# Inverse sums of the last pair of heads: spread by transfers in place of transposes on TensorE

## The chip, the cores and the metric

One core of a Trainium2 chip runs the kernel. The metric is the device time of one execution in microseconds (us); the time of a kernel is the median of several runs.

## What is computed

The reference is a decoder block with two attention branches that read one normalised input. Cut to what matters here:

```
h = rms_norm(x, norm_g)                              # x: 512 x 1024
fq, fk, fv, fz, mq, mk, mv, mz, ga, gb, fl = split(h @ w_in)
y_fox  = softmax(q k^T / 8 + c_i - c_j, causal) @ v * silu(fz)       # 8 heads of 64
y_moba = softmax(q k^T / 8 over selected blocks) @ v * silu(mz)      # 8 heads of 64
merged = sigmoid(ga + b_0) * (y_fox @ w_fox) + sigmoid(gb + b_1) * (y_moba @ w_moba)
out    = x + merged @ w_out
```

A softmax is an exponential divided by the sum of its row. The change concerns how the inverse of that sum reaches the outputs of two of the sixteen heads.

## The kernel before

Every product is made from operands split into a high and a low part, three matmuls for one. In the projections the activations are Gh and Gl and the weights wh and wl. The weights come by DMA from SP into four buffers (tag wr), ACT makes the high part (L140) and DVE the low part (L142), some products ahead of their use.

The sixteen heads are worked off in four groups of four: f/a, f/b, m/a, m/b (`attn_group`, L516). A group has two pairs of heads, and a head has these steps:

- `Aa` (L562): logits on PE (L571, L572), row maximum on DVE (L574), exponential with its row sum on ACT (L576). After the second head of a pair DVE inverts the sums into `ri` (L591), with the tokens on partitions.
- `Bb` (L609): PE transposes the exponentials (L616) into banks p_a, p_b and p_cc of tag tp, a ring of three; ACT and DVE split them (L622, L623); PE makes the outputs `pv` (L626, L627); ACT moves the half of `pv` that holds the low part of v (`ysh`, L651), and DVE adds it to the other half (L652). The outputs of a pair are one tile `ypair`, with the channels on partitions and the tokens along the row.
- `Yp` (L659): DVE multiplies `ypair` (L678) by a factor `zr`, which holds the gate ZS (silu) times the inverse sums; ACT and DVE split the result into yh and yl (L679, L680) for the projections by w_fox and w_moba.

`ypair` has the tokens along the row, so each inverse sum is needed on 64 partitions of its column. The kernel gets it there in two ways.

Seven of the eight pairs use transfers. In `sums_out` (L593), after the pair's first `Bb`, PE transposes the eight columns of `ri` into an 8x128 bank of tag tp (p_ri, L596), ACT scales it by a half (L598) and issues a write to DRAM (L599). In `sums_in` (L601) ACT issues two reads, each of which spreads one head's 512 values over 64 partitions of the tile `rinv_bc` (L606). In `Yp` GpSimd (POOL) multiplies that tile by ZS (L677).

The last pair of the last group (`last and pr`) does it otherwise, all in `Yp`: POOL copies each column of `ri` 64 times along the row (two instructions, L670, scaled by a half) into a tile rinv_w of tag u, PE transposes that tile in four pieces of 128x128 (L673) into a bank of tag lg, and DVE multiplies ZS by the bank (L674).

Around this stand the gate products. `Bb(2)` and `Bb(3)` of the last group, the tail of its list (L685), are followed by the unit wf3, and then by stage "gates" with the groups GA0, GA1 and GB0 (`group`, L722). A gate group is seven products (A11, S3, A12, S2, S1, A22, S4), each of 24 matmuls (two halves, four chunks, and three for one: L766, L768, L769). Four of the seven read sums S0 to S3 of blocks of the activations, which POOL loads back from DRAM at the start of the stage (`load_sums`, L286, eight loads at L290), into memory that the attention tiles give free. `Yp` of the last pair (`gate[0]`) is called after the third unit of GA0 (L1116).

The order on each engine isn't that of the program: a scheduler sets it with a simulated timeline, so instructions of different units are mixed. Each engine works its own list in order, and a waiting instruction holds up all behind it. DMAs are issued from the lists of SP, ACT and POOL.

Of the kernel before, what the change touches and what calls it, by code (L numbers as in the profile page):

```python
# [7 lines left out]
F32 = mybir.dt.float32  # L8
F32R = mybir.dt.float32r
AF = mybir.ActivationFunctionType  # L10
OP = mybir.AluOpType
AX = mybir.AxisListType

P = 128
S = 512
D = 1024
NT = S // P
KT = D // P
HD = 64
# [10 lines left out]
def fox_moba_kernel(ctx: ExitStack, tc, xT, x, w_in, w_fl, w_fox, w_moba, w_out, cst, rope, out):  # L30
# [3 lines left out]
    V, A, G, T = nc.vector, nc.scalar, nc.gpsimd, nc.tensor  # L34
# [6 lines left out]
    stage = {}  # L41
# [7 lines left out]
    def t2(tag, bufs, name, shape=(P, 512), dt=F32):  # L49
        pool = stage["pool"] if tag in ("qs", "pt", "pc", "ys") else sb  # L50
        return pool.tile(list(shape), dt, name=name, tag=tag, bufs=bufs)

    def pst(tag, bufs, name):
        return ps.tile([P, 512], F32, name=name, tag=tag, bufs=bufs)
# [4 lines left out]
    def tp(name):  # L59
        return pst("tp", 3, name)  # L60
# [30 lines left out]
    ident = con.tile([P, P], F32, name="ident")  # L91
# [134 lines left out]
    r = con.tile([P, NT], F32, name="r")  # L226
# [190 lines left out]
    ZS = {}  # L417
# [95 lines left out]
    ri = con.tile([P, 16, 4], F32, name="rinv")  # L513
    R_dram = dr.tile([16, NT, P], F32, name="r_dram")

    def attn_group(br, half, gq, gk):  # L516
        fox = br == "f"
        qn, kn = QN[f"{br}q{half}"], QN[f"{br}k{half}"]
        hb = 4 * (half == "b") + (0 if fox else 8)
        last = br + half == "mb"  # L520

        direct = br + half != "fa"
        st = {}
# [38 lines left out]
        def Aa(h):  # L562
            def go():
                qs, kh, kl, q2 = st[h]
                hh = hb + h
                pts = []
                for i in range(NT):
                    n = P * (i + 1)
                    lg = pst("lg", 2, "lg")
                    qt = slice(i * P, (i + 1) * P)  # L570
                    T.matmul(lg[:, :n], qs[:, qt], kh[:, :n], start=True, stop=False)  # L571
                    T.matmul(lg[:, :n], q2[:, qt], kl[:, :n], start=False, stop=True)  # L572
                    pt = stage["pool"].tile([P, n], F32, name=f"p{i}", tag=f"p{i}", bufs=2)
                    V.tensor_tensor_reduce(pt, lg[:, :n], mask[:, 512 - n:512], -0.125, 3.0e38,  # L574
                                           op0=OP.add, op1=OP.min, accum_out=mkn[:, hh, i:i + 1])
                    A.activation(pt, pt, AF.Exp, bias=mkn[:, hh, i:i + 1], scale=-1.0,  # L576
                                 accum_out=rs[:, hh, i:i + 1])
                    pts.append(pt)
                st[h] = pts
                if h % 2:  # L580
                    inverse_sums(h // 2)
                elif h:
                    sums_in(0)
            return go
# [8 lines left out]
        def sums_out(pr):  # L593
            h0 = hb + 2 * pr
            p = tp("p_ri")
            T.transpose(p[:8, :P], ri[:, h0:h0 + 2, :].rearrange("p h t -> p (h t)"), ident)  # L596
            rt = sb.tile([8, P], F32, name="rinv_t", tag="rinv_t", bufs=1)
            A.activation(rt, p[:8, :P], AF.Copy, scale=0.5)  # L598
            A.dma_start(out=R_dram[h0:h0 + 2].rearrange("h t p -> (h t) p"), in_=rt)  # L599

        def sums_in(pr):  # L601
            if last and pr:
                return
            rb = st["r", pr] = stage["pool"].tile([P, S], F32, name="rinv_bc", tag="rinv_bc", bufs=1)
            for o in range(2):
                A.dma_start(out=rb[o * HD:(o + 1) * HD, :],  # L606
                            in_=R_dram[hb + 2 * pr + o].rearrange("t p -> (t p)").partition_broadcast(HD))

        def Bb(h):  # L609
            def go():  # L610
                pts, vt = st[h], VT[f"{br}v{half}"]
                o = h % 2
                pv = pst("pv", 1, "pv")

                def blk(dst, i, j):
                    T.transpose(dst, pts[i][:, j * P:(j + 1) * P], ident)  # L616

                def spl(p, n):
                    tag, w, bufs = ("pt", 512, 4) if n == 512 else ("pc", 256, 2)
                    hi = t2(tag, bufs, "pth", (P, w), F32R)  # L620
                    lo = t2(tag, bufs, "ptl", (P, w), F32R)
                    A.activation(hi[:, :n], p[:, :n], AF.Copy)  # L622
                    V.tensor_tensor(out=lo[:, :n], in0=p[:, :n], in1=hi[:, :n].bitcast(F32), op=OP.subtract)  # L623
                    return hi, lo
                def pvm(j, hl, c0, n, start, stop):
                    T.matmul(pv[:, P * j:P * j + n], vt[:, j, h, :], hl[0][:, c0:c0 + n], start=start, stop=False)  # L626
                    T.matmul(pv[:, P * j:P * j + n], vt[:, j, h, :], hl[1][:, c0:c0 + n], start=False, stop=stop)  # L627
                pa = tp("p_a")
                for i in range(4):
                    blk(pa[:, i * P:(i + 1) * P], i, 0)  # L630
                pb = tp("p_b")
                for i in range(1, 4):
                    blk(pb[:, (i - 1) * P:i * P], i, 1)
                blk(pb[:, 384:512], 3, 3)
                ha = spl(pa, 512)
                hbb = spl(pb, 512)
                pc = tp("p_cc")
                for i in range(2, 4):
                    blk(pc[:, (i - 2) * P:(i - 1) * P], i, 2)
                hc = spl(pc, 256)  # L640
                pvm(0, ha, 0, 512, True, False)
                pvm(1, hbb, 0, 384, False, False)
                pvm(3, hbb, 384, 128, False, False)
                pvm(2, hc, 0, 256, False, True)
                pr = h // 2
                if o == 0:
                    st["y", pr] = t2("u", 4, "ypair") if last and pr else t2("ys", 1, "ypair")
                y = st["y", pr]
                me, ot = (slice(0, HD), slice(HD, P)) if o == 0 else (slice(HD, P), slice(0, HD))
                sh = t2("u", 4, "ysh")  # L650
                A.activation(sh[me, :], pv[ot, :], AF.Copy)  # L651
                V.tensor_tensor(out=y[me, :], in0=pv[me, :], in1=sh[me, :], op=OP.add)  # L652
                if o == 0 and not (last and pr):
                    sums_out(pr)
                elif pr:
                    sums_in(1)
            return go

        def Yp(pr):  # L659
            def go():  # L660
                y = st["y", pr]
                gp = 2 * (half == "b") + pr
                yh = t2("y", 15, f"yh{br}{gp}", dt=F32R)
                yl = t2("y", 15, f"yl{br}{gp}", dt=F32R)
                if last and pr:
                    zr, rb = ZS[br, gp], pst("lg", 2, "p_rinv")
                    h0 = hb + 2 * pr
                    rw = t2("u", 4, "rinv_w")
                    for o in range(2):
                        G.tensor_scalar(rw.rearrange("p (t o d) -> p t o d", o=2, d=HD)[:, :, o, :],  # L670
                                        ri[:, h0 + o, :, None].to_broadcast([P, NT, HD]), 0.5, None, op0=OP.mult)
                    for t in range(NT):
                        T.transpose(rb[:, t * P:(t + 1) * P], rw[:, t * P:(t + 1) * P], ident)  # L673
                    V.tensor_tensor(out=zr, in0=zr, in1=rb, op=OP.mult)  # L674
                else:
                    zr = st["r", pr]
                    G.tensor_tensor(out=zr, in0=ZS[br, gp], in1=zr, op=OP.mult)  # L677
                V.tensor_tensor(out=y, in0=y, in1=zr, op=OP.mult)  # L678
                A.activation(yh, y, AF.Copy)  # L679
                V.tensor_tensor(out=yl, in0=y, in1=yh.bitcast(F32), op=OP.subtract)  # L680
                Y[br, gp] = (yh, yl)
            return go
# [553 lines left out]
```

## Time and profile before

| | us |
|---|---|
| median of 3 runs | 425.06 |
| lowest, highest run | 424.13, 425.23 |
| profiled execution, its own time | 424.43 |
| its span | 422.5 |
| mean granted TensorE clock | 0.999 |

The profile shows one execution. PE is TensorE's matmuls, PEld its weight loads, DVE VectorE, ACT ScalarE, POOL GpSimd, SP the engine that only issues DMAs; ACTq is ACT's queue of DMA issues. In a timeline row stand the start in us, the length in us, the engine, the line, the operation, the output and inputs, and in brackets how long the engine was idle before and what released it. The chain that ended last has rows of start, length and instruction, each of them cut to what it adds to the chain. In the table of waits a row gives the total, the count and the longest wait in us. In the table of stretches the columns are the length, then busy time and count of PE, PEld, DVE, ACT and POOL, then the granted clock, the DMA share and GB/s.

### The profile page before, as it was taken

The numbers are of one execution on the slowest core, as the hardware profiler recorded it, in microseconds if no ns is written. First come the engines' busy times: TensorE is split into PE (matmuls) and PEld (weight loads), VectorE is DVE, ScalarE is ACT, GpSimd is POOL, SyncE is SP. The second block draws the span as 40 slices with busy tenths as digits, with TensorE's granted clock in tenths as the row PEclk, the third lists the DMA queues.
The fourth block names the chain that finished last, engine by engine and source line by source line (L and its number), as shares of the span: only waits on it lengthen the run. The fifth ranks groups of instructions, "written<-read, shape, count | busy, mean of one in ns | idle before, by whom it ended". The sixth has DMA issues, their size and how long they took to land.

```text
span 422.5 us, 7680 instructions
## 1 busy us (share of the span) xinstructions
PE 417.3 (99%) x2912; PEld 388.0 (92%) x2912; DVE 327.5 (78%) x575; ACT 279.7 (66%) x528; POOL 102.4 (24%) x120
## 2 busy tenths in 40 slices
PE   8999999999999999999999999999999999999996
PEld 6998899999999998899998888899999989988885
DVE  4669968799968779668666778767979698689883
ACT  5987327877877978569758687756655535686450
POOL 1067600224235550025650100340000000022230
PEclk9999999999999999999999999999999999999999
DMA  7982325567252123303122311673142603697494
GB/s 227 396 290 98 99 101 159 158 192 223 63 168 102 45 83 101 102 24 101 33 93 78 102 47 27 240 247 110 35 169 67 233 2 117 213 249 119 99 138 162
DMA packets 24484, 56.10 MB, mean 133 GB/s; under 512 B 2824, under 2 KB 7616, under 8 KB 24448
## 3 DMA queue, kind: packets, MB, share of 16 engines
q1 hardware_dynamic: 13536, 38.11, 28.0%
q0 software_dynamic: 3392, 8.39, 9.0%
q10 hardware_dynamic: 7520, 9.11, 6.8%
q8 instruction: 23, 0.38, 0.4%
q14 instruction: 13, 0.11, 0.1%
HBM read 48.11 MB, written 6.32 MB: 129 GB/s over the span
## 4 chain that ended last, share of the span: by engine, by line
PE 97%; DMA 1%; SPq 0%; DVE 0%; issue 0%
PE pb_GB L769 3%; PE pb_GA L769 3%; PE pb_GA L766 3%; PE pb_GB L766 3%; PE pb_GB L768 3%; PE pb_GA L768 3%; PE po L957 3%; PE po L956 3%; PE po L955 3%; PE pv L627 2%; PE lg L572 2%; PE pv L626 2%; PE lg L571 2%; PE pf L696 2%; PE pm L697 2%; PE pf L697 2%
## 5 line engine op out<-in xcount | busy, mean ns | idle before, releaser
L342 POOL TENSOR_TENSOR ff<-ss,mh 128x8 f32<-128x8 f32 x16 | 29.7, 1857 | 72.7 <-DVE ss L340 54.2
L576 ACT ACTIVATE p<-p,negm 128x128 f32<-128x128 f32 (+1 forms) x64 | 35.7, 558 | 13.0 <-DVE negm L574 12.0
L574 DVE CUSTOM_DVE_ANT_0 p<-lg,mask 128x128 f32<-128x128 f32 (+1 forms) x64 | 30.7, 485 | 15.0 <-PE lg L572 14.5
L904 POOL DMA_DIRECT2D wr_o<-in_w_out_dram x4 | 4.9, 1293 | 95.5 <-ACT wr_o L903 95.5
L142 DVE TENSOR_TENSOR wl_GA<-wr_ga,wh_GA 128x1024 fp32r<-128x1024 f32 x14 | 16.9, 1222 | 5.9 <-ACT wh_GA L140 3.9
L140 ACT ACTIVATE wh_GA<-wr_ga 128x1024 fp32r<-128x1024 f32 x14 | 14.6, 1059 | 10.1 <-PE pb_GA L768 5.1
L140 ACT ACTIVATE wh_GB<-wr_gb 128x1024 fp32r<-128x1024 f32 x14 | 14.6, 1059 | 9.5 <-PE pm L696 3.5
L571 PE MATMUL lg<-KH,QS 128*128 128x128 f32 (+1 forms) x64 | 20.4, 328 | 0.0
L918 DVE TENSOR_TENSOR wl_o<-wr_o,wh_o 128x1024 fp32r<-128x1024 f32 x14 | 17.0, 1219 | 3.8 <-ACT wh_o L917 3.8
L917 ACT ACTIVATE wh_o<-wr_o 128x1024 fp32r<-128x1024 f32 x14 | 14.8, 1060 | 7.6 <-PE pb_GB L768 2.8
L142 DVE TENSOR_TENSOR wl_GB<-wr_gb,wh_GB 128x1024 fp32r<-128x1024 f32 x14 | 16.9, 1221 | 3.5 <-ACT wh_GB L140 3.5
L652 DVE TENSOR_TENSOR ypair<-pv,ysh 64x512 f32<-64x512 f32 x16 | 11.0, 687 | 6.2 <-ACT ysh L651 5.8
L546 DVE SCALAR_TENSOR_TENSOR KL<-p_kT,cs,KH 64x512 fp32r<-64x512 f32 x16 | 12.0, 747 | 3.4 <-ACT KH L543 3.2
L623 DVE TENSOR_TENSOR ptl<-p_a,pth 128x512 fp32r<-128x512 f32 x16 | 10.9, 684 | 4.3 <-ACT pth L622 4.2
L651 ACT ACTIVATE ysh<-pv 64x512 f32<-64x512 f32 x16 | 9.5, 593 | 7.1 <-PE pv L627 4.7
L336 DVE TENSOR_REDUCE ss<-sq 128x8 f32<-128x512 f32 x16 | 10.8, 680 | 3.6 <-ACT sq L335 3.6
L766 PE MATMUL pb_GA<-Gh,wh_GA 128*128 128x256 f32 x48 | 13.5, 282 | 0.0
L768 PE MATMUL pb_GA<-Gl,wh_GA 128*128 128x256 f32 x48 | 13.5, 281 | 0.0
L769 PE MATMUL pb_GA<-Gh,wl_GA 128*128 128x256 f32 x48 | 13.5, 281 | 0.0
L769 PE MATMUL pb_GB<-Gh,wl_GB 128*128 128x256 f32 x48 | 13.5, 281 | 0.0
L768 PE MATMUL pb_GB<-Gl,wh_GB 128*128 128x256 f32 x48 | 13.4, 281 | 0.0
L766 PE MATMUL pb_GB<-Gh,wh_GB 128*128 128x256 f32 x48 | 13.3, 281 | 0.0
(461 smaller groups left out, 1794.1 us busy)
## 6 DMA issues: line engine op xcount, KB each, us to landing
wr_ga<-in_w_in_dram SPq DMA_DIRECT2D x8, 512.0 KB
wr_gb<-in_w_in_dram SPq DMA_DIRECT2D x8, 512.0 KB
wr_o<-in_w_out_dram SPq DMA_DIRECT2D x8, 512.0 KB
xt<-in_xT_dram SPq DMA_DIRECT2D x8, 256.0 KB
x<-in_x_dram SPq DMA_DIRECT2D x8, 256.0 KB
s_dramh<-sum_sh ACTq DMA_DIRECT2D x8, 256.0 KB
s_draml<-sum_sl ACTq DMA_DIRECT2D x8, 256.0 KB
wr_wf<-in_w_fox_dram SPq DMA_DIRECT2D x4, 512.0 KB
```

Source lines behind the costliest of these rows:

```text
L140: A.activation(hi[:, :, 0:n], src, AF.Copy)
L142: eng.tensor_tensor(out=lo[:, q, 0:n], in0=src[:, q], in1=hi[:, q, 0:n].bitcast(F32), op=OP.subtract)
L342: G.tensor_tensor(out=f2, in0=ss.rearrange("p t h -> p (t h)"), in1=mh, op=OP.pow)
L571: T.matmul(lg[:, :n], qs[:, qt], kh[:, :n], start=True, stop=False)
L574: V.tensor_tensor_reduce(pt, lg[:, :n], mask[:, 512 - n:512], -0.125, 3.0e38, op0=OP.add, op1=OP.min, accum_out=mkn[:, hh, i:i + 1])
L576: A.activation(pt, pt, AF.Exp, bias=mkn[:, hh, i:i + 1], scale=-1.0, accum_out=rs[:, hh, i:i + 1])
L697: T.matmul(p, lo[:, k, cc], yh, start=False, stop=(k == 3))
L766: T.matmul(o, hi[:, k, cc], lh, start=(n < 3 and c == 0 and k == 0), stop=False, skip_group_check=True)
L768: T.matmul(o, hi[:, k, cc], ll, start=False, stop=False, skip_group_check=True)
L769: T.matmul(o, lo[:, k, cc], lh, start=False, stop=(k == 3), skip_group_check=True)
L917: A.activation(wide(hi), wide(R[key, c]), AF.Copy)
L918: V.tensor_tensor(out=wide(lo), in0=wide(R[key, c]), in1=wide(hi).bitcast(F32), op=OP.subtract)
```

## The change

The last pair takes the same way as the other seven. `sums_out(1)` is called for it after `Bb(2)`, `sums_in(1)` after `Bb(3)`, and `Yp(1)` has only the branch with POOL's multiplication. The transposes of L673 and their bank, the two copies of L670 and the multiplication of L674 go. Its tile rinv_bc is taken from tag u of the pool that lasts the whole kernel, in the place of rinv_w.

```
         def sums_in(pr):
-            if last and pr:
-                return
-            rb = st["r", pr] = stage["pool"].tile([P, S], F32, name="rinv_bc", tag="rinv_bc", bufs=1)
+            rb = st["r", pr] = (t2("u", 4, "rinv_bc") if last and pr else
+                                stage["pool"].tile([P, S], F32, name="rinv_bc", tag="rinv_bc", bufs=1))
             for o in range(2):
                 A.dma_start(out=rb[o * HD:(o + 1) * HD, :],
                             in_=R_dram[hb + 2 * pr + o].rearrange("t p -> (t p)").partition_broadcast(HD))
...
-                if o == 0 and not (last and pr):
+                if o == 0:
                     sums_out(pr)
                 elif pr:
                     sums_in(1)
...
-                if last and pr:
-                    zr, rb = ZS[br, gp], pst("lg", 2, "p_rinv")
-                    h0 = hb + 2 * pr
-                    rw = t2("u", 4, "rinv_w")
-                    for o in range(2):
-                        G.tensor_scalar(rw.rearrange("p (t o d) -> p t o d", o=2, d=HD)[:, :, o, :],
-                                        ri[:, h0 + o, :, None].to_broadcast([P, NT, HD]), 0.5, None, op0=OP.mult)
-                    for t in range(NT):
-                        T.transpose(rb[:, t * P:(t + 1) * P], rw[:, t * P:(t + 1) * P], ident)
-                    V.tensor_tensor(out=zr, in0=zr, in1=rb, op=OP.mult)
-                else:
-                    zr = st["r", pr]
-                    G.tensor_tensor(out=zr, in0=ZS[br, gp], in1=zr, op=OP.mult)
+                zr = st["r", pr]
+                G.tensor_tensor(out=zr, in0=ZS[br, gp], in1=zr, op=OP.mult)
```

Behind the scheduler the lists differ only around this place. PE's list has four transposes (L673) less and one (L596) more, and the last head's transposes (L616) stand behind the outputs of the head before it and seven matmuls of GA0. ACT's has rinv_t, one write and two reads more, and yhm (L679) of the last pair stands ahead of one weight split (L140) and one copy of a bank (L776) that it stood behind. POOL's L677 stands where L670 stood. DVE's has L674 less, and L678 stands ahead of one weight split (L142) that it stood behind.

## The prediction

> **What bounds the kernel now.** I read the page first: the span, the busy shares, the span in 40 slices and the shares of the chain that ended last.
>
> ```profile
> span 422.5 us, 7680 instructions
> PE 417.3 (99%) x2912; PEld 388.0 (92%) x2912; DVE 327.5 (78%) x575; ACT 279.7 (66%) x528; POOL 102.4 (24%) x120
> PE   8999999999999999999999999999999999999996
> PE 97%; DMA 1%; SPq 0%; DVE 0%; issue 0%
> ```
>
> PE is busy in every slice between the first and the last and makes 97% of the chain. Busy alone doesn't prove that it is never held up, so the second view was the waits of PE, over the whole span:
>
> ```profile
> PE warm_ps L104 <- DVE fg_pre L479: 1.1, 1, 1.1
> PE fqa L390 <- DVE wh_fqa L163: 0.5, 1, 0.5
> ```
>
> These are all of them, and both belong to the first input tiles. From then on PE runs its list without a gap, and the chain is that list. Two things can therefore change the time: what PE has to issue, and a new wait of PE that isn't there now. Work taken from DVE, ACT or POOL is worth nothing by itself.
>
> **The change part by part.** *PE's own work.* Next come the chain's rows around the four removed transposes (start, us, what), and around one 8x128 transpose of another pair, of the kind that is added.
>
> ```profile
> 288.24 0.44 PE p_rinv L673 x4
> ...
> 255.84 0.23 PE pf L697
> 256.18 0.23 PE pf L695
> ```
>
> The four of L673 hold the chain for 0.44 us, 0.11 each. Around the 8x128 transpose (L596, which the chain leaves out as too short) one matmul ends at 255.84 + 0.23 = 256.07 and the next counts from 256.18: 0.11 for it. PE thus loses 0.44 and gains 0.11: **-0.33 us**. The Trainium skill (TensorE: Matmul & The Clock Gate, Part 4: PE-mode transpose) has a transpose inside a kernel at about 275 ns; by that the estimate would be -0.83 us. The chain's 0.44 for four speaks against it as a price on the path, since they overlap.
>
> *What the change moves on PE.* The order of the instructions, which a scheduler sets, shows more than the diff does. The added transpose takes the next bank of tag tp, a ring of three, so the last head's transposes (head 3, L616) slide back. Head 2's eight pv matmuls and seven of GA0's first product now stand ahead of them, then come the added transpose, p_a and p_b in a row, 15 gate matmuls, p_cc, 2 more, and head 3's pv. The rows that time this, of PE, ACT and DVE before:
>
> ```profile
> 275.10 0.28 PE L627 MATMUL pv<-ptl,v_mvb 128*128 128x256 f32 x1
> ...
> 278.72 0.40 PE L626 MATMUL pv<-pth,v_mvb 128*128 128x512 f32 x1
> ...
> 279.89 0.28 PE L627 MATMUL pv<-ptl,v_mvb 128*128 128x256 f32 x1
> ```
>
> ```profile
> 256.60 0.25 ACT L598 ACTIVATE rinv_t<-p_ri 8x128 f32<-8x128 f32 x1
> ...
> 275.53 0.60 ACT L651 ACTIVATE ysh<-pv 64x512 f32<-64x512 f32 x1
> ...
> 276.64 0.38 ACT L622 ACTIVATE pth<-p_cc 128x256 fp32r<-128x256 f32 x1
> ```
>
> ```profile
> 277.50 0.41 DVE L623 TENSOR_TENSOR ptl<-p_cc,pth 128x256 fp32r<-128x256 f32 x1
> ```
>
> With head 2's pv moved to the front (273.5 on, 1.3 us as head 3's take from 278.72 to 280.0), the added transpose falls at about 275.6, p_a and p_b end at 276.6, and p_cc ends at about 278.75 after 15 matmuls of 0.12. ACT does ysh (275.55 to 276.15), rinv_t (0.25), the issue of the write, two pth (to 277.8), then the pth of p_cc from 278.8 (0.38); DVE's ptl (0.41) is ready near 279.65. PE wants it for its last pv matmul, now near 280.0. A margin of 0.35 us: I cost this at nothing, and if it breaks it costs what it is over by, 0.5 us at most, as ACT has nothing else longer than that in between.
>
> *POOL.* Two copies of the sums go (L670) and one multiplication comes (L677), both behind the loads of S0 to S3 in POOL's order.
>
> ```profile
> 263.09 1.29 POOL L677 TENSOR_TENSOR rinv_bc<-zs_mzb,rinv_bc 128x512 f32<-128x512 f32 x1 [22.67 <-DMA rinv_bc<-r_dram]
> ...
> 276.03 0.54 POOL L290 DMA_DIRECT2D S2l<-s_draml  x1 [5.44 <-PE p_cc L616]
> ...
> 279.42 0.54 POOL L290 DMA_DIRECT2D S3l<-s_draml  x1 [2.33 <-PE pv L626]
> 279.98 2.67 POOL L670 TENSOR_SCALAR rinv_w<-rinv 128x256 f32<-128x256 f32 x2
> ```
>
> S2l waits for p_cc, so it goes out near 279 and not at 276.03, and S3h and S3l follow by 280.2. To land such a load takes:
>
> ```profile
> S2l<-s_draml POOLq DMA_DIRECT2D x1, 512.0 KB, 5.7
> S3h<-s_dramh POOLq DMA_DIRECT2D x1, 512.0 KB, 6.4
> ```
>
> S2l is there by 285, S3h and S3l by 286.6. PE first reads S2l at 292.16 (row below) and S3 later still: 5 us or more to spare, so nothing. After L677 POOL has no work before the output stage.
>
> *The transfers.* ACT gets rinv_t (0.25), a write of 4 KB and two reads of 128 KB. The reads stand behind ysh of head 3, which waits for pv to end; with pv over at about 280.3, the first goes out near 281.0. The write is out by 276.7, over 4 us earlier, so the reads don't wait for it. From the first read's issue to POOL's multiplication the seven other pairs give 3.6 to 5.5 us; the quickest and the slowest:
>
> ```profile
> 152.34 1.10 ACTq L606 DMA_DIRECT2D rinv_bc<-r_dram  x2
> ...
> 155.93 1.30 POOL L677 TENSOR_TENSOR rinv_bc<-zs_fzb,rinv_bc 128x512 f32<-128x512 f32 x1 [0.59 <-DMA rinv_bc<-r_dram]
> ...
> 176.20 1.11 ACTq L606 DMA_DIRECT2D rinv_bc<-r_dram  x2
> ...
> 181.73 1.28 POOL L677 TENSOR_TENSOR rinv_bc<-zs_fzb,rinv_bc 128x512 f32<-128x512 f32 x1 [20.25 <-DMA rinv_bc<-r_dram]
> ```
>
> So POOL starts between 284.6 and 286.5. I take 286.5, the upper end, because the engines of the DMA are fuller here than there (busy times by stretch; the last two columns are DMA share and GB/s):
>
> ```profile
> 278.00:282.00 4.00, 4.00 (x33) 3.90 (x32) 1.92 (x2) 2.25 (x3) 2.55 (x3) 1.00 0.99 346
> ...
> 176.00:182.00 6.00, 6.00 (x50) 5.86 (x49) 4.64 (x10) 4.66 (x12) 0.27 (x1) 1.00 0.46 131
> ```
>
> *The new waits and who stands behind them.* DVE loses L674 but its L678 now waits for POOL, with a weight split (L142) behind it; ACT's yhm (L679) waits for that L678, and behind yhm stands the split that starts group GA1.
>
> ```profile
> 286.87 1.23 DVE L142 TENSOR_TENSOR wl_GA<-wr_ga,wh_GA 128x1024 fp32r<-128x1024 f32 x1 [1.49 <-ACT wh_GA L140]
> 288.71 0.69 DVE L674 TENSOR_TENSOR zs_mzb<-zs_mzb,p_rinv 128x512 f32<-128x512 f32 x1 [0.62 <-PE p_rinv L673]
> 289.43 0.69 DVE L678 TENSOR_TENSOR ypair<-ypair,zs_mzb 128x512 f32<-128x512 f32 x1
> ```
>
> ```profile
> 289.11 1.06 ACT L140 ACTIVATE wh_GA<-wr_ga 128x1024 fp32r<-128x1024 f32 x1 [1.80 <-issue]
> ...
> 290.56 0.62 ACT L679 ACTIVATE yhm<-ypair 128x512 fp32r<-128x512 f32 x1
> ```
>
> ```profile
> 291.81 0.28 PE L766 MATMUL pb_GA<-Gh,wh_GA 128*128 128x256 f32 x1
> 291.93 0.28 PE L768 MATMUL pb_GA<-Gl,wh_GA 128*128 128x256 f32 x1
> 292.05 0.28 PE L766 MATMUL pb_GA<-S2h,wh_GA 128*128 128x256 f32 x1
> 292.16 0.28 PE L768 MATMUL pb_GA<-S2l,wh_GA 128*128 128x256 f32 x1
> ```
>
> The row at 291.81 is the first use of that split; with 0.33 less ahead of it PE is there at 291.5. Backwards from it: split 1.06, yhm 0.62, L678 0.69, POOL 1.29 and some 0.2 of hand-over make 3.9, so PE waits if POOL starts after **287.6**. At 286.5 there is 1.1 us left; L678 then runs from 287.9 and yhm from 288.6, and the split starts at 289.2 in place of 289.11. The DVE split behind L678 slips from 286.87 to 288.6; its chunk belongs to the product on S3, after 297, so that costs nothing. The bank of tag lg that goes free is wanted by nobody before the output stage.
>
> *Sum.* 424.43 (the profiled execution: 422.5 of span and 1.93 around it) - 0.33 = 424.1. That execution lies 0.63 under the median of the runs, 425.06; the same step from the median gives 425.06 - 0.33 = **424.7 us**, which I forecast.
>
> **The rivals.**
>
> *The reads land late (slower).* Place: L678 on DVE. For it: DMA at 0.99 of its time and 346 GB/s from 278 to 282, and the three S loads that now go out just ahead of the reads. Against it: even a 512 KB load lands in 6.4 us, and 281.0 + 6.4 = 287.4 is still inside the point of 287.6. The Trainium skill (DMA: Bandwidth & Descriptors, Queues, rings and completion order) has each DMA engine drain a whole packet of one queue before it turns to the next, and a completion signal that goes out only after all earlier writes of that engine; that would tie the small reads to the big loads ahead of them. As a mechanism of this kernel: the reads end with S3l, issued at 280.0 and landing at 286.4, or, with the weight load that is also under way (512 KB at 346 GB/s, 1.5 us), at 287.9. The first costs nothing, the second 0.3 us: 425.0. For every microsecond past 287.6 the kernel loses one; to be slower by over 0.3% (1.28 us, about what a measurement of this kernel can tell from no change) the reads must cost 1.6 us, so POOL must start at 289.2, 8.2 us after the issue. At 290, 9 us after it, the loss is 2.4 and the time 425.06 - 0.33 + 2.4 = 427.1.
>
> *Head 3's chain breaks.* PE waits for the ptl of p_cc because rinv_t and the write's issue stand ahead of ACT's pth. For it: the margin of 0.35. Price up to 0.5: 425.2.
>
> *Faster than the sum.* That DVE's 0.69 and POOL's 1.4 (2.67 - 1.29) show up in the time. Against it: PE waits for neither. The most that PE itself could give is the whole 0.44, or 424.6; 0.3% (423.8) would take a saving that no row shows.
>
> **How the numbers follow.** No new wait, 424.7: 0.58. Reads late, but under the 1.6 us, around 425.3: 0.14. Reads late by more, 426.4 to 428: 0.15, more than the rows give, because the crowd of 278 to 284 has no like among the seven other pairs. Head 3's chain: 0.08, a quarter of it with more behind it than I see. Faster by over 0.3%: 0.05. So faster 0.05, within 0.3% 0.78, slower 0.17. The range goes from 423.8 (the lowest run before, 424.13, less 0.33) to 426.8, which takes in the mild delays and the start of the bad one.
>
> **What would show it.** Right: PE has no wait between 273 and 300, the chain holds no L673 and one more L596, POOL's last L677 starts by 287.6 and S2l goes out near 279. The head-3 step is wrong if PE waits for ptl near 280; the reads' step if DVE's L678 idles beyond 289 on POOL and PE waits for wh_GA near 291.5. The prediction as a whole is wrong if PE waits anywhere else, or if the same list of matmuls takes PE another time.

## Result and profile after

The changed kernel takes **424.04 us** (median of 20 runs, 423.6 to 424.39) against 424.72 (20 runs, 424.13 to 425.54) of the kernel before in the same comparison: ratio 0.9983, 95% interval 0.9977 to 0.999. That is 0.68 us faster (0.16%), inside the 0.3% that the forecast counted as the same. The profiled execution took 423.67 us, with a span of 421.9.

The page of the changed kernel, the lines that answer to those of before:

```profile
span 421.9 us, 7677 instructions
PE 416.7 (99%) x2909; PEld 387.6 (92%) x2909; DVE 326.8 (77%) x574; ACT 280.4 (66%) x529; POOL 101.7 (24%) x119
PE 97%; DMA 1%; SPq 0%; DVE 0%; issue 0%
```

PE has three instructions less (four transposes gone, one added) and is still the whole chain. All its waits, over the span:

```profile
PE warm_ps L104 <- DVE fg_pre L479: 1.1, 1, 1.1
PE fqa L390 <- DVE wh_fqa L163: 0.5, 1, 0.5
PE fqa L390 <- ACT Zh L130: 0.3, 1, 0.3
```

All three stand in the first 13 us, at the first input tiles. The third is not in the list of before, yet PE is no later behind it; where the change is, the list has no wait. Lines behind L662 stand 12 lower than before: POOL's multiplication is L665 (L677), the product with the factor L666 (L678), yhm L667 (L679), the reads L605 (L606). PE's timeline of the changed kernel, around the added transpose, at the first use of GA1's split, at the first use of S2 and at its end:

```profile
275.56 0.27 PE L596 MATMUL p_ri<-ident,rinv 128*8 128x128 f32 x1
275.67 0.60 PE L615 MATMUL p_a<-ident,p 128*128 128x128 f32 x4
...
278.32 0.38 PE L615 MATMUL p_cc<-ident,p 128*128 128x128 f32 x2
...
279.94 0.28 PE L626 MATMUL pv<-ptl,v_mvb 128*128 128x256 f32 x1
...
291.44 0.28 PE L754 MATMUL pb_GA<-Gh,wh_GA 128*128 128x256 f32 x1
...
291.68 0.28 PE L754 MATMUL pb_GA<-S2h,wh_GA 128*128 128x256 f32 x1
...
418.30 0.28 PE L945 MATMUL po<-wh_o,mg 128*128 128x256 f32 x1
```

The same last matmul before:

```profile
418.67 0.28 PE L957 MATMUL po<-wh_o,mg 128*128 128x256 f32 x1
```

The split's first use was at 291.81 and is at 291.44, S2's was at 292.05 and is at 291.68, the last matmul was at 418.67 and is at 418.30: **0.37 us** earlier in each, and nothing is given back in between. A matmul shortly ahead of the change (pf<-ylf, 272.34 before, 272.32 after) is already 0.02 earlier, so the changed stretch itself gives 0.35.

The span has shrunk by more than that; the rest lies behind the last matmul. There SP, which issues the last store (419.44 before, 419.07 after), works off a closing list of waits, among them the one for the landing of that store. Its entries ahead of the landing and from it on, first of the kernel before and then of the changed one (count, shortest, median and longest in ns, then when the first and the last start):

```profile
L1232 SPq EVENT_SEMAPHORE  x4: 27/28/28, 419.8 to 420.2; - x4
L1232 SPq EVENT_SEMAPHORE  x5: 28/28/28, 421.3 to 421.6; - x5
```

```profile
L1220 SPq EVENT_SEMAPHORE  x7: 28/28/28, 419.5 to 419.9; - x7
L1220 SPq EVENT_SEMAPHORE  x2: 28/28/28, 421.0 to 421.0; - x2
```

Before, four entries pass ahead of the landing and five from it on; after, seven and two. The entries start 0.06 us apart, so the three that now pass while SP waits anyway are worth 0.18. By the traces the end of the span comes 3.80 us behind the start of the last matmul before and 3.63 after: **0.17 us**, and with PE's 0.37 that is 0.54 of span.

The chain of the factor, on POOL, ACT and DVE of the changed kernel:

```profile
276.92 0.54 POOL L290 DMA_DIRECT2D S2l<-s_draml  x1 [6.35 <-PE p_b L615]
279.48 0.54 POOL L290 DMA_DIRECT2D S3l<-s_draml  x1
287.19 1.28 POOL L665 TENSOR_TENSOR rinv_bc<-zs_mzb,rinv_bc 128x512 f32<-128x512 f32 x1 [7.17 <-DMA rinv_bc<-r_dram]
```

```profile
280.26 1.11 ACTq L605 DMA_DIRECT2D rinv_bc<-r_dram  x2
...
289.23 0.63 ACT L667 ACTIVATE yhm<-ypair 128x512 fp32r<-128x512 f32 x1 [1.86 <-DVE ypair L666]
289.77 1.04 ACT L140 ACTIVATE wh_GA<-wr_ga 128x1024 fp32r<-128x1024 f32 x1
```

```profile
279.16 0.42 DVE L622 TENSOR_TENSOR ptl<-p_cc,pth 128x256 fp32r<-128x256 f32 x1 [0.60 <-ACT pth L621]
...
288.50 0.69 DVE L666 TENSOR_TENSOR ypair<-ypair,rinv_bc 128x512 f32<-128x512 f32 x1 [3.08 <-POOL rinv_bc L665]
```

POOL starts at 287.19, 6.9 us after the issue of the first read. The split begins at 289.77, ends at 290.81 and feeds the matmul at 291.44. So the spare time that the forecast put at 1.1 us was 0.6.

### The profile page after: what moved, and what is told of

It is laid out like the page before. It is cut to its first block, busy times and chain, and to the rows that moved or that the text cites. A ratio compares the mean times of both kernels' runs of the same rounds, so it can differ in the third digit from the quotient of the medians.

```text
span 421.9 us, 7677 instructions
## 1 busy us (share of the span) xinstructions
PE 416.7 (99%) x2909; PEld 387.6 (92%) x2909; DVE 326.8 (77%) x574; ACT 280.4 (66%) x529; POOL 101.7 (24%) x119
## 4 chain that ended last, share of the span: by engine, by line
PE 97%; DMA 1%; SPq 0%; DVE 0%; issue 0%
PE pb_GB L757 3%; PE pb_GA L757 3%; PE pb_GB L754 3%; PE pb_GA L756 3%; PE pb_GB L756 3%; PE pb_GA L754 3%; PE po L945 3%; PE po L944 3%; PE po L943 3%; PE pv L626 2%; PE lg L572 2%; PE pv L625 2%; PE lg L571 2%; PE pf L684 2%; PE pf L683 2%; PE pf L685 2%
## 5 line engine op out<-in xcount | busy, mean ns | idle before, releaser
L140 ACT ACTIVATE wh_GB<-wr_gb 128x1024 fp32r<-128x1024 f32 x14 | 14.6, 1059 | 10.1 <-PE pm L684 3.5
L142 DVE TENSOR_TENSOR wl_GB<-wr_gb,wh_GB 128x1024 fp32r<-128x1024 f32 x14 | 16.9, 1223 | 3.9 <-ACT wh_GB L140 3.9
L142 DVE TENSOR_TENSOR wl_GA<-wr_ga,wh_GA 128x1024 fp32r<-128x1024 f32 x14 | 16.9, 1222 | 2.8 <-ACT wh_GA L140 2.3
L140 ACT ACTIVATE wh_GA<-wr_ga 128x1024 fp32r<-128x1024 f32 x14 | 14.6, 1057 | 5.9 <-PE pb_GA L756 2.7
```

What stands on the lines that cost most here:

```text
L140: A.activation(hi[:, :, 0:n], src, AF.Copy)
L142: eng.tensor_tensor(out=lo[:, q, 0:n], in0=src[:, q], in1=hi[:, q, 0:n].bitcast(F32), op=OP.subtract)
```

## Experiments

Two theories stood against each other at first. The first: the time is PE's list and PE's waits, and nothing else. The rival: the work taken from DVE and POOL shows in the time as well. Then came the question how near the reads are to costing something, and what sets their time.

**1. The changed kernel again**, to see how its schedule scatters. No edit.

> The changed kernel once more, beside the kernel before on the same chip. Theory A (only PE's list counts: four transposes less, one more): PE's last matmul comes 0.33 to 0.37 us earlier and the time is 0.35 us lower, so the 0.68 between the medians of the first 20 runs is half noise. Theory B (something outside PE's list, such as the landing of the last store, also became shorter): the time is again 0.6 to 0.7 us lower while PE's last matmul is only 0.37 earlier.

Measured: 424.0 (11 runs, 423.59 to 424.67) against 424.5 before, ratio 0.9991 (0.9982 to 1.0). Its profiled execution took 424.51, in the upper part of its runs, and shows why. POOL and PE there:

```profile
288.29 1.28 POOL L665 TENSOR_TENSOR rinv_bc<-zs_mzb,rinv_bc 128x512 f32<-128x512 f32 x1 [8.01 <-DMA rinv_bc<-r_dram]
```

```profile
291.59 0.27 PE L757 MATMUL pb_GA<-Gh,wl_GA 128*128 128x256 f32 x1
291.96 0.38 PE L754 MATMUL pb_GA<-Gh,wh_GA 128*128 128x256 f32 x1
292.18 0.28 PE L756 MATMUL pb_GA<-Gl,wh_GA 128*128 128x256 f32 x1
```

The reads landed so that POOL started at 288.29, and the split ended at 291.91. Its first use comes 0.37 behind its neighbour where 0.12 is usual: 0.25 held. The list of PE's waits doesn't have this, because the row of the matmul before ends only at 291.86; the weight load for the first use (PEld, 0.30 idle on this split) shows it. There is a second hold, which the forecast didn't follow. Behind the split ACT copies a bank (e_GA, L764) into which the product on S2 goes:

```profile
292.45 0.19 PEld L754 LDWEIGHTS pb_GA<-S2h,wh_GA 128*128 128x128 f32 x1 [0.19 <-ACT e_GA L764]
```

The matmul at 292.45 comes 0.27 behind its neighbour, 0.15 more than usual, and the matmul behind each hold starts after 0.22 in place of 0.12. These four parts make 0.6. At its last matmul PE is 0.88 later than in the first profile, and 0.26 of it were there from the start. The forecast's first rival, the reads landing late, is therefore real: it cost this execution some 0.6 us. Of the expectation's two theories both hold in part: PE's list gives 0.35, and the closing list of SP the 0.17 that lie outside it (3.62 in this profile too).

**2. Before, without the four transposes.** DVE multiplies by rinv_w itself; the last pair's factor is then not transposed. POOL's two copies and DVE's multiplication stay.

```diff
-                    zr, rb = ZS[br, gp], pst("lg", 2, "p_rinv")
+                    zr = ZS[br, gp]
...
-                    for t in range(NT):
-                        T.transpose(rb[:, t * P:(t + 1) * P], rw[:, t * P:(t + 1) * P], ident)
-                    V.tensor_tensor(out=zr, in0=zr, in1=rb, op=OP.mult)
+                    V.tensor_tensor(out=zr, in0=zr, in1=rw, op=OP.mult)
```

> The kernel before, with the four transposes (L673) left out and DVE multiplying by POOL's tile of copied columns itself, so the factor of the last pair of heads is wrong: its columns are not transposed. DVE, POOL and ACT keep all their work and no transfer is added. Theory A: PE's list is shorter by 0.44 us and the time too: 0.44 below before, 0.1 below the changed kernel. Rival C (the gain came from DVE's 0.69 or POOL's 1.4 us that the change takes away): no gain, same as before.

Measured: 423.87 (11 runs), ratio 0.9988 (0.9979 to 0.9997). Its last matmul:

```profile
418.23 0.28 PE L955 MATMUL po<-wh_o,mg 128*128 128x256 f32 x1
```

That is 0.44 before the 418.67 of the kernel before: the four transposes at 0.11, and this with DVE's and POOL's work in place. The closing list of SP is that of the kernel before (3.80), as no transfer was added. The rival falls: the work that went from those two engines bought nothing on the path.

**3. One more pass of POOL over the factor.**

```diff
+                z4 = zr.rearrange("p (t q) -> p t q", q=P)
+                for _ in range(1 if last and pr else 0):
+                    G.tensor_tensor(out=z4, in0=z4, in1=ones[:, None, :].to_broadcast([P, NT, P]), op=OP.mult)
```

> The changed kernel with one more pass of POOL over the last pair's factor (times ones, some 1.3 us), every other engine's order unchanged. By the changed kernel's trace yhm starts at 289.23 and the split of GA1 at 289.77, which PE needs at 291.44 and gets at 290.8. Theory A with the margin as the prediction had it: POOL's result comes 1.3 later, beyond the point, yhm at 290.5, split done at 292.1, PE waits 0.6 to 0.8 us there and the kernel is 0.7 slower than the changed one, 0.1 to 0.3 slower than before. Rival D (the transfers are hidden by several us): the same as the changed kernel.

Measured: 425.2 (12 runs, 424.16 to 429.38), ratio 1.0013 (1.0004 to 1.0022), 1.2 over the 424.0 of run 1. The pass costs more than the 0.7 by which it was expected to pass the point. The profiled execution was the slowest, 429.38, 4.2 over the median, and so shows the bad case and not the usual one; its waits and its stretches show what a long wait does:

```profile
PE pb_GA L757 <- ACT wh_GA L140: 3.8, 1, 3.8
```

```profile
288.00:291.00 3.00, 3.00 (x27) 3.00 (x27) 0.00 (x0) 0.00 (x0) 0.72 (x1) 1.00 0.13 49
295.00:297.00 2.00, 1.70 (x8) 1.52 (x9) 1.97 (x3) 1.98 (x3) 0.00 (x0) 0.76 0.51 164
297.00:300.00 3.00, 3.00 (x18) 3.00 (x17) 2.50 (x3) 1.63 (x4) 0.00 (x0) 0.59 0.17 66
```

From 288 to 290.3 DVE, ACT and POOL all stand still: all three stand in line behind the reads, POOL starts at 290.28, and PE stops for 3.8 us where the forecast's chain says. Then the granted clock (the third column from the right) is 0.76 and 0.59, and from 297 to 300 PE has 18 matmuls in place of the 28 of the first profile.

**4. Two more passes.** The same edit with 2. Here the scheduler put the product with the factor behind one more split on DVE, and yhm behind GA1's split on ACT.

> The changed kernel with two more passes of POOL (2.6 us). Here the scheduler puts yhm behind the split of GA1 on ACT and L678 behind one more weight split on DVE. Theory A: though POOL is later than with one pass, nothing that PE needs soon stands behind the late factor, so PE doesn't wait and the time is that of the changed kernel, within 0.1. Rival E (what counts is when the factor is ready): slower than with one pass, by 1.3 us more.

Measured: 425.13 (11 runs), ratio 1.0019 (1.0011 to 1.0028). The expectation missed: PE had a wait, on another instruction.

```profile
PE pb_GA L757 <- DVE uGA L770: 1.2, 1, 1.2
```

With yhm out of the way of the split, the next in line is DVE's addition uGA, which empties the bank that the product on S3 writes. It stood behind the product with the factor, which began at 292.86, and ran at 296.34. The chain that the forecast followed was the first that breaks, not the only one.

**5. The factor pinned later, and nothing else.** The order of run 4 written out by hand (`behind(e)` issues an instruction behind the last one of engine e), without extra passes.

```diff
-                G.tensor_tensor(out=zr, in0=ZS[br, gp], in1=zr, op=OP.mult)
-                V.tensor_tensor(out=y, in0=y, in1=zr, op=OP.mult)
-                A.activation(yh, y, AF.Copy)
+                def on(e):
+                    return behind(e) if last and pr else ExitStack()
+                with on(E.Pool):
+                    G.tensor_tensor(out=zr, in0=ZS[br, gp], in1=zr, op=OP.mult)
+                with on(E.DVE):
+                    V.tensor_tensor(out=y, in0=y, in1=zr, op=OP.mult)
+                with on(E.Activation):
+                    A.activation(yh, y, AF.Copy)
...
-        if n == 2:
+        if n == 3:
```

> The changed kernel, transfers untouched, but the use of the late factor stands further back: L678 one weight split later on DVE, yhm behind the split of GA1 on ACT. Theory A2 (PE's list is 0.33 shorter, and the changed kernel gives part of it back in those executions in which the reads land after POOL's point of 287.6 to 287.9): the reads land as late as before, POOL between 287 and 290.5, but PE waits nowhere behind 12 us; PE's last matmul 0.33 to 0.44 earlier than before, time 0.4 to 0.9 below before and not above the changed kernel. Rival F (the late reads cost nothing in the changed kernel either; its second profile is an exception): the same time as the changed kernel, within 0.1.

Measured: 423.92 (11 runs) against 424.63 before, ratio 0.9985 (0.9976 to 0.9993); 423.64 in the profiled execution, no wait, PE's last matmul at 418.31. By time it isn't to be told from the changed kernel. A second profile of it:

> Control for the other three on the same chip: POOL's product at 286.5 to 288.3 as in the three profiles of this schedule so far, PE without a wait and 0.37 ahead of the kernel before, 423.6 to 424.5.

```profile
288.29 1.28 POOL L670 TENSOR_TENSOR rinv_bc<-zs_mzb,rinv_bc 128x512 f32<-128x512 f32 x1 [8.26 <-DMA rinv_bc<-r_dram]
```

This time POOL started at 288.29, as late as in run 1, and the execution took 423.66 with PE's last matmul at 418.32: the same lateness that cost run 1 0.6 us costs nothing here, though PE runs 0.25 earlier here and would have been held longer in the changed kernel's order.

**6. Twelve more transposes**, unread, of 128x128, in one piece of PE's list of kernel 5.

```diff
+                    idle = pst("lg", 2, "p_idle")
+                    with behind(mybir.EngineType.PE):
+                        for t in range(12):
+                            c = slice((t % 4) * P, (t % 4 + 1) * P)
+                            T.transpose(idle[:, c], ZS[br, gp][:, c], ident)
```

> As r_factor_pinned_later, with 12 more transposes of 128x128 in a bank that nobody reads. It prices a transpose on the path. Theory A: 0.11 us each, 1.3 us over r_factor_pinned_later, 0.4 to 1.0 above before. Rival (the 0.27 us of one transpose's row is its price): 3.3 us over r_factor_pinned_later.

Measured: 425.16 (11 runs), 1.24 over the 423.92 of kernel 5; ratio to before 1.0013 (1.0004 to 1.0021). The chain:

```profile
288.75 0.12 PE pb_GA L770
288.87 1.31 PE p_idle L674 x12
290.18 0.12 PE pb_GA L767
```

1.31 for twelve is 0.11 each, the price that the forecast took from its row for four, and the times agree with it. The 275 ns of the Trainium skill (TensorE: Matmul & The Clock Gate, Part 4: PE-mode transpose) would make 3.3 us of them; as a price on the path it falls here.

**7. The loads of S3 behind the factor.** As kernel 5, and the two S3 loads go out only behind POOL's product.

```diff
+        for i in range(3):
+            load_sum(i)
...
+            with behind(mybir.EngineType.Pool):
+                load_sum(3)
```

> As r_factor_pinned_later, and the two loads of S3 (512 KB each) are issued by POOL behind its multiplication and no more ahead of it, so they don't travel with the two reads. Theory G (the reads are late because they share the DMA engines with the S loads): they land within 5.5 us of their issue as for the other pairs, so POOL starts by 286 in place of 287.2 to 290.3. Rival H (they are late by themselves, or because of the weight loads): 6.9 to 10 us as before. Time: that of r_factor_pinned_later, unless S3 comes too late for its product at 297: issued at 287 and 6.5 us to land make 294, so no wait.

Measured: 423.96 (11 runs), ratio 0.9984 (0.9975 to 0.9992). A second profile of it (423.98 us):

> The same kernel as the one whose two S3 loads go out behind POOL's product, looked at once more because its second read took 2 us to issue in the first look. Theory that the reads end with the crowd ahead of them: with the S3 loads out of the way POOL starts at 284 to 285.8, 3.6 to 5.5 us after the issue of the first read at 280.3, if the second read is issued in its usual 0.5 us. Rival, no dependence on the S3 loads: 286.5 or later again.

The two reads and POOL in the second profile:

```profile
280.60 2.08 ACTq L609 DMA_DIRECT2D rinv_bc<-r_dram  x2
```

```profile
287.42 2.22 POOL L674 TENSOR_TENSOR rinv_bc<-zs_mzb,rinv_bc 128x512 f32<-128x512 f32 x1 [9.62 <-DMA rinv_bc<-r_dram]
```

In both profiles the two reads took over 2 us to issue (1.10 elsewhere), and POOL began at 287.36 and 287.42, 6.8 to 6.9 us after the first issue. The expectation of 284 to 285.8 missed: taking away the two loads that stand just ahead of the reads doesn't bring POOL's start forward. Why the issue takes longer then, no run shows. What moved on the queues (packets, MB, share; q0 has POOL's loads, q1 SP's weight loads, q10 ACT's transfers) shows why it need not help: in the changed kernel from 280.3 to 283.2, and in the first profile of this run from 282 to 283 and from 283 to 284:

```profile
q0 software_dynamic: 266, 0.98, 93.7%
```

```profile
q10 hardware_dynamic: 69, 0.11, 31.8%
...
q1 hardware_dynamic: 82, 0.34, 99.2%
q10 hardware_dynamic: 2, 0.00, 1.0%
```

In the changed kernel nothing of the reads moves for the 3 us behind their issue. Without the S3 loads about half of the reads moves from 282 to 283, but then the weight load that SP issues 1.1 us behind the first read (at 281.55) has the transfers almost to itself, and the other half follows only behind 284. The expectation had named the weight loads in its rival; no run moves one away, so how much of the 6.9 us they alone would cause is not shown.

**8. Two more copies in the crowd.** As kernel 5, with two copies of 512 KB from DRAM to DRAM right behind the last S load on POOL's queue.

```diff
+        for d, t in zip(S_dram, S_copy):
+            with behind(mybir.EngineType.Pool):
+                nc.gpsimd.dma_start(out=t, in_=d[3])
```

> As the kernel with the factor pinned later, with two further 512 KB copies from DRAM to DRAM issued on POOL's queue right behind the last S load, so that they stand in front of or beside the two reads of the inverse sums. Theory that the reads end with the crowd of transfers issued ahead of them: 1 MB more at 264 to 320 GB/s is 3.3 to 4 us more, so that POOL's product starts at 290 to 291.5 in place of 286.7; DVE's product and all that stands behind it comes that much later, and PE waits 0 to 1.5 us near 297 for the bank that DVE's addition frees: 424 to 425.5. Rival, that the time of the reads is a fixed chain of issue, write and read that does not depend on what else is under way: POOL starts at 286.5 to 287.5 as without the copies, PE has no wait and the time is 423.9, that of the pinned kernel.

Measured: 427.4 (6 runs, 425.91 to 428.28), ratio 1.0064 (1.0049 to 1.008). POOL, ACT's issue, PE's wait, and the landing of the second copy (the last number of its row) in the fastest of the runs, the profiled one:

```profile
280.41 0.50 POOL L294 DMA_DIRECT2D s_copyl<-s_draml  x1
290.45 1.29 POOL L674 TENSOR_TENSOR rinv_bc<-zs_mzb,rinv_bc 128x512 f32<-128x512 f32 x1 [9.55 <-DMA rinv_bc<-r_dram]
```

```profile
280.16 1.10 ACTq L609 DMA_DIRECT2D rinv_bc<-r_dram  x2
```

```profile
PE pb_GA L765 <- ACT wh_GA L140: 1.3, 2, 0.9
```

```profile
s_copyl<-s_draml POOLq DMA_DIRECT2D x1, 512.0 KB, 9.2
```

The reads, issued at the same time as ever, are there 10.3 us later, 2.2 to 3.8 us behind kernel 5: POOL's start was as expected, the price was higher (425.9 to 428.3 against 424 to 425.5). That the reads take a fixed time falls. PE's wait came not near 297 but at a third place, near 301, at a split behind DVE's delayed work. What the other runs, up to 2.4 us slower than the profiled one, lost beside this is not shown.

**9. The sums written column by column.** As kernel 5, without p_ri: the inverse sums go to DRAM straight from `ri`, 1024 pieces of 4 bytes (DVE doubles the sums before the inverse, in place of ACT's half), and the reads are issued after `Bb(2)`.

```diff
+            if last and pr:
+                A.dma_start(out=R_dram[h0:h0 + 2].rearrange("h t p -> p h t"), in_=ri[:, h0:h0 + 2, :])
```

> As r_factor_pinned_later, and for the last pair the inverse sums are written to DRAM straight from their tile, column by column (1024 elements of 4 bytes), behind the inversion; no transpose, no bank of tag tp and no copy, and the two reads are issued after head 2 and not after head 3. PE's list has no transpose for this pair at all. Theory A: 0.44 below before and 0.11 below r_factor_pinned_later, head 3's transposes back at 273.5. Rival I: the write of single elements takes so long that ACT, which waits for it ahead of the reads, holds up the splits behind them: PE waits between 276 and 284, slower than before.

Measured: 426.91 (6 runs), ratio 1.0057 (1.0042 to 1.0071). ACT and PE:

```profile
272.51 0.39 ACTq L595 DMA_DIRECT2D r_dram<-rinv  x1
...
285.70 1.10 ACTq L611 DMA_DIRECT2D rinv_bc<-r_dram  x2
286.85 1.06 ACT L140 ACTIVATE wh_GA<-wr_ga 128x1024 fp32r<-128x1024 f32 x1 [9.79 <-PE pb_GA L772]
```

```profile
PE pb_GA L769 <- ACT e_GA L779: 3.3, 1, 3.3
```

The reads are issued 13.2 us behind the write for which they wait, and since they are issued from ACT's list, ACT stands still with them: 9.8 us idle up to the split that follows them (the row names PE as what ended it, but the reads stand between). The same kernel with the reads and `Yp` moved behind the eighth unit of the gates (`n == 7`):

> The inverse sums of the last pair are written to DRAM column by column from the 128-row tile as soon as they exist, at about 272.5, without any transpose on PE; the two reads back and the product with the factor come only behind the eighth block of the gate's fill, far behind the 13.2 us that the write took in the run where the reads were issued too early. Theory that the time is PE's list alone: PE's rows stand 0.44 earlier than in the kernel before from 288.6 to the end (the four transposes, none added), PE has no wait, and the time is 0.07 to 0.1 under that of the kernel with the factor pinned later and 0.44 under the kernel before by the trace; by medians 0.44 to 0.75 under it, as in the earlier runs, where the medians differed by 0.1 to 0.35 more than PE's rows. Rival: the 1024 small pieces disturb the loads of the S tiles, which land from 280 to 287, and PE waits at the first use of an S tile, or ACT is again held at the reads: a listed wait of PE and 425 or more.

Measured: 423.86 (11 runs), ratio 0.9987 (0.9978 to 0.9995); no wait, though the S loads under way with the write (S2h to S3l) now took 9.6 to 11.1 us to land. The reads and POOL:

```profile
297.54 1.10 ACTq L611 DMA_DIRECT2D rinv_bc<-r_dram  x2
```

```profile
301.01 1.56 POOL L679 TENSOR_TENSOR rinv_bc<-zs_mzb,rinv_bc 128x512 f32<-128x512 f32 x1 [20.78 <-DMA rinv_bc<-r_dram]
```

```profile
297.00:301.00 4.00, 4.00 (x36) 4.00 (x35) 3.97 (x4) 1.39 (x4) 0.00 (x0) 1.00 0.18 66
```

At a DMA share of 0.18 the same reads take 3.5 us. The 0.1 us that the missing p_ri should give is below what the medians tell apart, but the trace shows it. From the matmul ahead of the change (272.61 here) to the last (418.51) PE takes 145.90, where the kernel before takes 146.33, kernel 5 145.99 and run 2 145.90: 0.43 less for four transposes without the one, 0.34 with it.

## Why the prediction was right

*The bound and the sum.* Right. PE's list is the chain, no wait was added, and PE's changed stretch is 0.35 shorter where -0.33 was forecast. Run 2 gives the removed part by itself (0.44), run 6 the price of one transpose at both ends of the sum (0.11).

*The base.* The forecast was 0.66 above the result. 0.34 of that is the base: the median of three runs, 425.06, against 424.72 for twenty of the same kernel, and 424.5 to 424.63 in the later comparisons. From the profiled execution's 424.43 the sum was 424.1, within 0.06 of the measured median, but that is luck: from the median of twenty it would have been 424.39, 0.35 above the result.

*What is left.* The sum had no term behind PE's last matmul, and there 0.17 was gained: the change issues three transfers more (one write, two reads), and the last store stands three places further back in SP's closing list, so that three entries fewer, at 0.06 each, come behind its landing. What sets the places no run tried. All twelve profiles with a write and two reads for the last pair have 3.62 to 3.63 from the start of the last matmul to the end of the span, the kernel before and run 2 have 3.80. With PE's 0.37 that makes 0.54. By medians the kernel gained 0.68, 0.50 and (kernel 5) 0.71 us, and the intervals of all three (0.42 to 0.98 the first) hold 0.54. So the gain is accounted for within what the runs tell apart; the 0.17 was not foreseen.

*PE's order and head 3's chain.* Right: p_ri at 275.56 (275.6 forecast), ptl of p_cc ready at 279.16 + 0.42 = 279.58 (279.65), PE there at 279.94 (280.0). The margin was 0.36, and no run with this order shows a wait of PE there.

*POOL's queue.* S2l went out at 276.92 and not near 279: it waits for p_b, no longer for p_cc. S3h and S3l were out by 280.0 (280.2 forecast). This cost nothing, as said, but the step had the wrong releaser.

*The reads.* This is the term that was mis-sized. "So POOL starts between 284.6 and 286.5": it started at 287.19, and in the six other profiles with the same transfers (runs 1, 3, 4, 5 twice, 6) at 286.68 to 290.28, 6.4 to 10.1 us after the issue. The range came from seven pairs that read in quieter stretches (0.46 of the DMA's time where one was quoted, against 0.92 from 280 to 284 and 0.90 from 284 to 288 here). In these seven profiles POOL's start follows the last large transfer that is issued ahead of the reads: in the changed kernel S3l was issued at 279.48 and took 6.5 us, to 286.0, and POOL started 1.2 later; over the seven the gap is 1.1 to 1.7, while POOL's start moves by 3.6. With two copies more POOL starts 0.9 after the second copy has landed, at 290.45. The rule of the Trainium skill (DMA: Bandwidth & Descriptors, Queues, rings and completion order) that was weighed as a rival has each DMA engine take whole packets of one queue in turn and complete a transfer only behind its earlier writes. Reads that end with the large loads agree with it; the taking of turns is not seen in the first 3 us behind the issue, in which POOL's queue alone moves. Run 7 shows that S3l is not the cause alone: without the S3 loads POOL starts as late, now behind the weight load.

*The point from which it costs.* 287.6 was near. In the changed kernel the chain from POOL's start to the end of the split took 3.62 and the matmul could follow 0.05 later, in place of the 3.9 that was added up, so the point is 291.44 - 3.67 = 287.8; in run 1 the same rule gives 288.04, and POOL's 288.29 is over it by the 0.25 that PE was held. "For every microsecond past 287.6 the kernel loses one" was too low: those 0.25 cost 0.62 in all, because the copy of the bank behind the split holds PE a second time and each hold has its after-effect, and the extra pass cost 1.2 where 0.7 was expected. Nor was DVE's slip harmless without limit: runs 4 and 8 show uGA and the next split behind the late factor. The late reads were given 0.14 and 0.15. In the changed kernel they cost one of the two profiled executions 0.6 us; in its medians they don't show, as it gained 0.68 and 0.50 where kernel 5, which lets the reads be late, gained 0.71. That "no new wait" came out in the first profile is in part luck: the range was too early by 0.7, the margin of 1.1 bore it, and in four of the seven profiles POOL's start lay past the point (288.29 twice, 288.80, 290.28).

## What to carry to other kernels

- When one engine's list is the whole chain, price a change by what that list gains or loses, at the rate at which those instructions stand in a row (0.11 us for a transpose here), and look at the rest only for new waits; then look behind the last instruction too, where 0.17 us of this case's gain lay.
- A time for a small transfer that was taken from quieter stretches can be far too short for a crowded one (3.6 to 5.5 us there, 6.4 to 10.1 here): look at which large transfers are in flight where it goes out, and expect it about when the last of them ends.
- When a late value stands in in-order lists, follow every instruction behind it, on each engine, until its user has time to spare; with the consumers one unit later (kernel 5), POOL's start 0.5 us past the old point of 287.8 cost nothing.

## What the runs showed of the hardware beside this

- The two longest stops of PE cost more than themselves: after 3.8 us (run 3) the granted clock was 0.76 from 295 to 297 and 0.59 from 297 to 300; after the 3.3 us of run 9 the stretch from 291 to 295 had 0.62 (24 matmuls where 36 is usual). After the 1.2 us of run 4 the clock stayed at 1.00.

```profile
291.00:295.00 4.00, 4.00 (x24) 4.00 (x24) 2.30 (x3) 2.07 (x4) 1.28 (x1) 0.62 0.74 241
```

- A write of 4 KB in 1024 pieces of 4 bytes (run 9) let the reads behind it go only 13.2 us after its issue, and the four 512 KB loads beside it (S2h to S3l) took 9.6 to 14.1 us to land, against 4.0 to 9.2 in the other profiles of the changed way.
